# Choice of experts: two operands of the choosing arithmetic move from SBUF to PSUM

## The chip, the cores and the metric

The kernel runs on one core of a Trainium2 chip. The metric is the device time of one execution in microseconds (us). Before the change three timed runs gave 3245.78, 3250.35 and 3260.03 us, so the median is 3250.35 us. The profiled execution, from which every duration in this document comes unless another is named, took 3240.46 us; its span, from the first instruction to the last, is 3238.8 us.

Five engines work side by side, each on its own queue in program order, and meet at semaphores: PE (TensorE, matrix products), DVE (VectorE), ACT (ScalarE), POOL (GpSimd) and SP, which only issues transfers. PEld is the weight load of PE. SBUF is the working memory, PSUM the small memory into which PE writes.

## The reference

One decoder layer runs for 256 prompt tokens and 64 sample tokens: a mixer, attention over memory, and a feed-forward layer called PEER, which is where the change lies. The part of the reference that matters:

```python
q = (xt @ wq).reshape(T, PEER_HEADS, 2, PEER_HALF)          # 8 heads, 2 halves
s = jnp.einsum('thid,hikd->thik', q, sub_keys)              # 128 scores for each half
s1, i1 = lax.top_k(s[:, :, 0], K)                           # K = 16
s2, i2 = lax.top_k(s[:, :, 1], K)
comb = (s1[..., :, None] + s2[..., None, :]).reshape(T, PEER_HEADS, K * K)
cid = (i1[..., :, None] * PEER_NKEYS + i2[..., None, :]).reshape(T, PEER_HEADS, K * K)
sf, pos = lax.top_k(comb, K)
eid = jnp.take_along_axis(cid, pos, axis=-1)                # 16 of 16384 experts per head
g = jax.nn.softmax(sf, axis=-1)
act = gelu(einsum('td,tkd->tk', x, u[eid]))                 # rows of peer_u
out = einsum('tk,tkd->td', g * act, v[eid])                 # rows of peer_v
```

## The kernel before, in words

For the prompt tokens the kernel does not gather experts. It multiplies the 256 tokens with all 16384 rows of `peer_u` (the u stage, 128 row blocks of 128 experts, four units of four matrix tiles each), takes the gelu, multiplies with a gate that is zero for experts not chosen, and multiplies with all rows of `peer_v` (the v stage). For the 64 sample tokens it gathers the chosen rows and works on DVE.

**A unit of the u stage** passes four engines. DVE transposes a piece of a row block (L1837, into a tile `tt`, five of which exist), ACT rounds it to the high part `H` (L1846), POOL subtracts to get the low part `L` (L1849; a few of them are done by DVE, L1852), and PE does twelve matrix products (L1865 to L1867). Seven `H` and seven `L` tiles exist, so PE can be some units behind.

**The choice of experts** is a side task, `choose`, that runs in the first half of the u stage, between units. A stream object calls it a little at a time: after each unit it advances each side generator by its rate (0.254 steps per unit for this one), so the order of the instructions on PE, DVE, ACT and POOL is fixed when the program is written down, from counts and from a table of assumed costs (`run("dve", 2.6)` and the like), not from measured times. Only SP's order is left to a scheduler. `choose` treats three blocks of 128 rows in turn, the sample tokens (block 2) and then the two halves of the prompt (0 and 1). For each block:

- L1636 copies the key indices into PSUM as floats. L1640 and L1641 form the sums of first and second maxima, `comb`, 136 per head (the pairs that can be among the sixteen best).
- L1541 to L1549 pick the best sixteen of each head.
- L1656 to L1666 turn a position into the index of the first and of the second maximum (`pf`).
- L1668 compares each of the 128 indices of a token (8 heads of 16) with sixteen whole numbers, which gives the one-hot `oh` of 2048 elements per partition. L1672 multiplies by the key indices, L1676 sums. This happens twice per block (i = 0 and 1), six times in all.
- L1682 to L1687 form the softmax weights.

Once block 2 is done, the sample gathers start: POOL issues an indirect transfer (L1722) for each of 64 slots, and DVE takes the dot products (L1729). Once block 1 is done, the gates of the prompt begin (L1750, L1771).

`PP["n128"]`, `PP["row"]` and `PP["IF"]` are three parts of one bank of PSUM, `n128p` in the profile: the numbers 0, -1, ..., -127 in each partition, a scratch row of 128 elements, and the key indices of a block. `t8` gives one of three large tiles in SBUF, shared by `comb`, `oh` and the gathered rows `gu`. The tile `i16` (`i` in the profile) holds 0 to 15 in SBUF; the maxima `M` lie in `SS`, also in SBUF.

## Time and profile before

| | |
|---|---|
| timed runs | 3245.78, 3250.35, 3260.03 us |
| profiled execution / its span | 3240.46 / 3238.8 us |
| PE busy in the span | 3153.9 us (97%) |
| DVE, ACT, POOL busy | 2351.8, 1631.6, 1350.3 us |
| u stage (first load of a row block to last L1837) | about 1680 to 2505 us |
| `choose` (first L1640 to last L1687) | 1744.5 to 2050.5 us |

A row of the timeline gives start, duration, engine, line, operation, `out<-in`, shapes and the count of merged instructions; in brackets the idle time before it and what ended it. A row of waits gives the engine and line that waited, what it waited for, the sum in us, how often, and the longest. A row of windows gives the stretch, its length, the busy time (and instructions) of PE, PEld, DVE, ACT and POOL, the granted PE clock, the busy share of the DMA engines and GB/s. A row of a line's instructions gives min/median/max of the duration in ns.

### The profile page before, as it was taken

How to read it: one execution, taken by the hardware profiler on the slowest of the kernel's cores; microseconds unless marked ns; L12 is line 12 of the kernel's file. 1: busy time of each engine (PE TensorE's matmuls, PEld its weight loads, DVE VectorE, ACT ScalarE, POOL GpSimd, SP SyncE). 2: the span in 40 equal slices, each digit the busy share in tenths (PEclk: the TensorE clock that was granted, in tenths of full speed). 3: DMA queues.
4: the chain of work that ended last, by engine and by line, in shares of the span. 5: the costliest groups of instructions: out<-in, count | busy, mean ns of one | idle time of the engine just before them, and what ended most of it. 6: DMA issues, size and time to landing. Idle time of an engine off the chain costs nothing.

```text
span 3238.8 us, 57523 instructions
## 1 busy us (share of the span) xinstructions
PE 3153.9 (97%) x20589; PEld 2939.9 (91%) x20589; DVE 2351.8 (73%) x4548; ACT 1631.6 (50%) x3219; POOL 1350.3 (42%) x1439
## 2 busy tenths in 40 slices
PE   8999999999999999889999999999999999999997
PEld 6789999999999998869999999999999888888886
DVE  5556766666575557786687899987885788888885
ACT  5545543333454445555435444666665555555554
POOL 0011211111100001330138988988888555556653
PEclk9999999999999999999999999999999999999998
DMA  7668899888999998775786688878998999999995
GB/s 255 204 202 296 282 309 298 293 298 292 317 320 312 309 298 190 222 215 195 189 217 219 234 289 298 306 285 295 327 326 292 311 336 347 329 354 325 341 311 191
DMA packets 475371, 909.29 MB, mean 281 GB/s; under 512 B 40607, under 2 KB 286535, under 8 KB 449572
## 3 DMA queue, kind: packets, MB, share of 16 engines
q1 hardware_dynamic: 352972, 562.95, 52.5%
q0 software_dynamic: 54528, 208.44, 19.0%
q10 hardware_dynamic: 67584, 134.23, 12.2%
q8 instruction: 161, 2.64, 0.3%
q14 instruction: 126, 1.03, 0.1%
HBM read 849.41 MB, written 190.05 MB: 321 GB/s over the span
## 4 chain that ended last, share of the span: by engine, by line
PE 42%; POOL 2%; issue 2%; DVE 2%; DMA 1%; ACT 1%; SPq 0%; DVEq 0%; POOLq 0%; ACTq 0%
PE acc L2021 7%; PE acc L2022 7%; PE acc L2020 7%; PE pu L1867 6%; PE pu L1866 6%; PE pu L1865 6%; POOL L L1849 2%; PE pgate L1771 2%; DVE tt L1837 0%; PE pg L369 0%; PE pg L371 0%; PE pg L370 0%; DVE gu L1729 0%; DMA gain<-in_norm_final_dram 0%; DMA at<-act_d 0%
## 5 line engine op out<-in xcount | busy, mean ns | idle before, releaser
L251 DVE TENSOR_TENSOR L<-W,H 128x512 fp32r<-128x512 f32 x1320 | 914.1, 718 | 362.5 <-ACT H L250 346.2
L250 ACT ACTIVATE H<-W 128x512 fp32r<-128x512 f32 x1320 | 798.5, 625 | 683.9 <-PE pg L370 231.3
L1849 POOL TENSOR_TENSOR L<-tt,H 128x512 fp32r<-128x512 f32 x509 | 652.7, 1311 | 82.3 <-ACT H L1846 73.6
L1867 PE MATMUL pu<-XP,L 128*128 128x256 f32 x2048 | 582.7, 285 | 12.3 <-POOL L L1849 12.2
L369 PE MATMUL pg<-AH,H 128*128 128x320 f32 (+1 forms) x1872 | 587.9, 314 | 0.0
L1865 PE MATMUL pu<-XP,H 128*128 128x256 f32 x2048 | 585.7, 286 | 1.2 <-ACT H L1846 1.2
L1866 PE MATMUL pu<-XP,H 128*128 128x256 f32 x2048 | 579.9, 283 | 0.0
L371 PE MATMUL pg<-AH,L 128*128 128x320 f32 (+1 forms) x1872 | 579.1, 309 | 0.0
L370 PE MATMUL pg<-AL,H 128*128 128x320 f32 (+1 forms) x1872 | 578.9, 309 | 0.0
L1837 DVE STREAM_TRANSPOSE tt<-W 128x512 f32<-128x512 f32 x512 | 337.6, 690 | 115.9 <-POOL L L1849 108.4
L1867 PEld LDWEIGHTS pu<-XP,L 128*128 128x128 f32 x2048 | 392.7, 192 | 16.1 <-POOL L L1849 15.8
L2020 PE MATMUL acc<-H,wt 128*128 128x512 f32 x1024 | 398.5, 389 | 2.5 <-ACT H L250 2.5
L2021 PE MATMUL acc<-L,wt 128*128 128x512 f32 x1024 | 398.6, 389 | 0.3 <-DVE L L251 0.2
L2022 PE MATMUL acc<-H,wt 128*128 128x512 f32 x1024 | 398.4, 389 | 0.0
L1865 PEld LDWEIGHTS pu<-XP,H 128*128 128x128 f32 x2048 | 393.5, 192 | 1.6 <-ACT H L1846 1.4
L1866 PEld LDWEIGHTS pu<-XP,H 128*128 128x128 f32 x2048 | 393.2, 192 | 0.0
L1846 ACT ACTIVATE H<-tt 128x512 fp32r<-128x512 f32 x512 | 306.9, 625 | 154.9 <-DVE tt L1837 127.8
L369 PEld LDWEIGHTS pg<-AH,H 128*128 128x128 f32 (+1 forms) x1872 | 350.9, 187 | 4.5 <-issue 2.4
L370 PEld LDWEIGHTS pg<-AL,H 128*128 128x128 f32 (+1 forms) x1872 | 351.0, 188 | 2.3
L371 PEld LDWEIGHTS pg<-AH,L 128*128 128x128 f32 (+1 forms) x1872 | 350.7, 187 | 0.6
L1969 POOL TENSOR_TENSOR at<-at,G 128x108 f32<-128x108 f32 x192 | 166.6, 881 | 264.1 <-DMA at<-act_d 226.1
L2020 PEld LDWEIGHTS acc<-H,wt 128*128 128x128 f32 x1024 | 192.3, 188 | 42.7 <-ACT H L250 2.9
(489 smaller groups left out, 5334.7 us busy)
## 6 DMA issues: line engine op xcount, KB each, us to landing
u_d<-in_peer_u_dram ACTq DMA_DIRECT2D x128, 1024.0 KB
W<-u_d SPq DMA_DIRECT2D x128, 1024.0 KB
W<-in_peer_v_dram SPq DMA_DIRECT2D x256, 512.0 KB
W<-in_w_in_dram SPq DMA_DIRECT2D x176, 512.0 KB
W<-in_w_out_dram SPq DMA_DIRECT2D x64, 512.0 KB
W<-in_w_mem_k_dram SPq DMA_DIRECT2D x32, 512.0 KB
W<-in_w_mem_v_dram SPq DMA_DIRECT2D x32, 512.0 KB
W<-in_w_mem_q_dram SPq DMA_DIRECT2D x32, 512.0 KB
```

The costliest lines, as they stand in the source:

```text
L250: S.activation(h, src, AF.Copy)
L251: V.tensor_tensor(l, src, h.bitcast(F32), ALU.subtract)
L369: PE.matmul(out, hv[:, j, c0:c1], ah[:, k, 0:n], start=st, stop=False)
L370: PE.matmul(out, hv[:, j, c0:c1], al[:, k, 0:n], start=False, stop=False)
L371: PE.matmul(out, lv[:, j, c0:c1], ah[:, k, 0:n], start=False, stop=sp)
L1849: G.tensor_tensor(l, src, h.bitcast(F32), ALU.subtract)
L1865: PE.matmul(pu[:, 0:TP], hv[:, j], PP["xp"][:, 0, k], start=k == 0, stop=False)
L1866: PE.matmul(pu[:, 0:TP], hv[:, j], PP["xp"][:, 1, k], start=False, stop=False)
L1867: PE.matmul(pu[:, 0:TP], lv[:, j], PP["xp"][:, 0, k], start=False, stop=k == KC - 1)
L2020: PE.matmul(out, th, h, start=i == 0, stop=False)
L2021: PE.matmul(out, th, l, start=False, stop=False)
L2022: PE.matmul(out, tl, h, start=False, stop=i == P - 1)
```

## The change

The tile `i16` and the instruction that fills it are gone. L1668 compares with a slice of `n128` in PSUM instead; since that holds negative numbers, `pf` is formed with its sign turned (and, for i = 0, shifted by one, which the slice's start makes up for). For the sums, the sixteen second maxima of each head are first copied into the scratch row in PSUM, a new instruction per block, and L1640 and L1641 read them there. The assumed costs of the table stay as they were.

```diff
-    i16 = cst.tile([P, 16], F32, name="i16")
-    G.iota(i16, pattern=[[1, 16]], base=0, channel_multiplier=0, allow_small_or_imprecise_dtypes=True)
@@
             comb = t8("comb")[:, 0:8 * 136].rearrange("p (h n) -> p h n", h=8)
-            V.tensor_tensor(comb[:, :, 0:16], mv[:, :, 0, 0:1].broadcast_to([P, 8, 16]), mv[:, :, 1], ALU.add)
+            second = PP["row"].rearrange("p (h k) -> p h k", k=16)
+            V.tensor_copy(second, mv[:, :, 1])
+            V.tensor_tensor(comb[:, :, 0:16], mv[:, :, 0, 0:1].broadcast_to([P, 8, 16]), second, ALU.add)
             V.tensor_tensor(comb[:, :, 16:].rearrange("p h (a b) -> p h a b", b=8),
                             mv[:, :, 0, 1:].unsqueeze(3).broadcast_to([P, 8, 15, 8]),
-                            mv[:, :, 1, 0:8].unsqueeze(2).broadcast_to([P, 8, 15, 8]), ALU.add)
+                            second[:, :, 0:8].unsqueeze(2).broadcast_to([P, 8, 15, 8]), ALU.add)
@@
                 if i == 0:
                     V.tensor_copy(row, row.bitcast(U32))
-                    V.tensor_scalar(pfv, row, 1.0, -1.0, op0=ALU.max, op1=ALU.add)
+                    V.tensor_scalar(pfv, row, 1.0, -1.0, op0=ALU.max, op1=ALU.mult)
                 else:
-                    V.tensor_scalar(pfv, row, 1.0, -8.0, op0=ALU.is_gt, op1=ALU.mult)
+                    V.tensor_scalar(pfv, row, 1.0, 8.0, op0=ALU.is_gt, op1=ALU.mult)
                     V.tensor_tensor(row, row, pfv, ALU.mult)
-                    V.tensor_tensor(pfv, row, po, ALU.add)
+                    V.tensor_tensor(pfv, row, po, ALU.subtract)
                 oh = t8("oh").rearrange("p (h a b) -> p h a b", h=8, a=16)
                 V.tensor_tensor(oh, pf.unsqueeze(3).broadcast_to([P, 8, 16, 16]),
-                                i16.unsqueeze(1).unsqueeze(1).broadcast_to([P, 8, 16, 16]), ALU.is_equal)
+                                PP["n128"][:, 1 - i:17 - i].unsqueeze(1).unsqueeze(1).broadcast_to([P, 8, 16, 16]), ALU.is_equal)
```

The order of instructions on PE and ACT is the same as before. On DVE, at the place where block 1 forms its sums, the rows before the change are these (`SS` holds the maxima, `gu` a gathered row, `DOT` its dot product):

```order
L1837 STREAM_TRANSPOSE tt<-W 128x512 x4
L1852 TENSOR_TENSOR L<-tt,H 128x512
L1636 CAST n128p<-SS 128x256
L1640 TENSOR_TENSOR comb<-SS 128x8x16
L1641 TENSOR_TENSOR comb<-SS 128x8x120
L1837 STREAM_TRANSPOSE tt<-W 128x512 x2
```

With the change the same place reads as follows; lines have moved, since two were taken out near the top and two put in here (what was L1636 is L1634).

```order
L1837 STREAM_TRANSPOSE tt<-W 128x512 x4
L1852 TENSOR_TENSOR L<-tt,H 128x512
L1634 CAST n128p<-SS 128x256
L1639 COPY n128p<-SS 128x128
L1640 TENSOR_TENSOR comb<-SS,n128p 128x8x16
L1641 TENSOR_TENSOR comb<-SS,n128p 128x8x120
L1837 STREAM_TRANSPOSE tt<-W 128x512 x2
```

One copy has come in, and both sums now have one source in PSUM. Blocks 2 and 0 show the same. On SP the order has moved at one place of the u stage, where the stores of the gelu's results (`act_d`) and the loads of row blocks (`W`) alternate. Before:

```order
L1873 DMA act_d<-at 128x256
L1819 DMA W<-u_d_97 128x2048
L1873 DMA act_d<-at 128x256 x2
L1819 DMA W<-u_d_97 128x2048
L1873 DMA act_d<-at 128x256
```

With the change (the numbers in the names of tensors are two lower throughout):

```order
L1873 DMA act_d<-at 128x256 x2
L1819 DMA W<-u_d_95 128x2048
L1873 DMA act_d<-at 128x256
L1819 DMA W<-u_d_95 128x2048
L1873 DMA act_d<-at 128x256
```

The two stores that follow each other do so one row block earlier, so one load has been put behind one store.

## The prediction

> **What bounds the kernel now.** I read the page's busy times first, then the busy times in stretches of the u stage, then PE's waits, and then the timelines of DVE, POOL and PE around each wait. The columns of a stretch are its length, the busy time of PE, PEld, DVE, ACT and POOL, the granted clock, DMA share and GB/s.
>
> ```profile
> PE 3153.9 (97%) x20589; PEld 2939.9 (91%) x20589; DVE 2351.8 (73%) x4548; ACT 1631.6 (50%) x3219; POOL 1350.3 (42%) x1439
> ...
> 1800.00:1850.00 50.00, 50.00 (x419) 50.00 (x418) 42.48 (x79) 25.35 (x48) 46.29 (x36) 1.00 0.67 226
> 1900.00:1950.00 50.00, 45.08 (x364) 43.83 (x364) 47.98 (x89) 25.32 (x47) 47.35 (x38) 1.00 0.85 296
> 1950.00:2000.00 50.00, 47.39 (x388) 46.57 (x387) 48.22 (x146) 20.77 (x39) 44.38 (x37) 1.00 0.85 314
> 2000.00:2050.00 50.00, 44.46 (x349) 43.10 (x348) 48.15 (x74) 20.03 (x37) 43.23 (x35) 0.97 0.75 268
> ...
> 2100.00:2200.00 100.00, 100.00 (x846) 100.00 (x845) 81.37 (x158) 63.87 (x157) 85.51 (x70) 1.00 0.79 286
> ...
> PE pu L1867 <- POOL L L1849: 12.2, 14, 2.4
> PE pu L1865 <- ACT H L1846: 1.2, 1, 1.2
> ...
> PE acc L2020 <- ACT H L250: 2.5, 1, 2.5
> ```
>
> PE is the bound over the whole, but not from 1900 to 2057 us. There DVE is busy for 144.4 of 150 us (47.98 + 48.22 + 48.15) while PE loses time. The first two rows of waits are all of PE's waits between 1740 and 2060 us: 12.2 + 1.2 = 13.4 us in 15 waits. The last is the one wait of size after 2060 us, at the change to the v stage; so what PE gains here is kept to the end. Of the three blocks that are chosen, only the last two fall into this stretch; under block 2, from 1744 to 1836 us, PE never waits (all 15 waits end after 1900 us, and the stretch from 1800 to 1850 us has PE busy throughout), so nothing saved there counts.
>
> **What DVE is late with.** In pairs: an instruction that the change touches, POOL's run of subtractions at that moment (merged, with its count), and PE's wait a little later.
>
> ```profile
> 1889.52 6.24 DVE L1668 TENSOR_TENSOR oh<-pf,i 128x2048 f32<-128x2048 f32 x1
> 1889.83 3.77 POOL L1849 TENSOR_TENSOR L<-tt,H 128x512 fp32r<-128x512 f32 x3
> 1902.58 0.39 PE L1867 MATMUL pu<-XP,L 128*128 128x256 f32 x1 [2.36 <-POOL L L1849]
> ...
> 1949.21 4.43 DVE L1640 TENSOR_TENSOR comb<-SS 128x128 f32<-128x128 f32 x1
> 1948.47 5.02 POOL L1849 TENSOR_TENSOR L<-tt,H 128x512 fp32r<-128x512 f32 x4
> 1960.92 0.39 PE L1867 MATMUL pu<-XP,L 128*128 128x256 f32 x1 [1.73 <-POOL L L1849]
> ...
> 2003.41 7.95 DVE L1668 TENSOR_TENSOR oh<-pf,i 128x2048 f32<-128x2048 f32 x1
> 2002.92 6.29 POOL L1849 TENSOR_TENSOR L<-tt,H 128x512 fp32r<-128x512 f32 x5
> 2012.72 1.27 POOL L1849 TENSOR_TENSOR L<-tt,H 128x512 fp32r<-128x512 f32 x1 [3.52 <-ACT H L1846]
> 2012.70 0.38 PE L1865 MATMUL pu<-XP,H 128*128 128x256 f32 x1 [1.20 <-ACT H L1846]
> 2014.05 0.49 PE L1867 MATMUL pu<-XP,L 128*128 128x256 f32 x1 [0.85 <-POOL L L1849]
> 2017.58 0.38 PE L1867 MATMUL pu<-XP,L 128*128 128x256 f32 x1 [0.69 <-POOL L L1849]
> ```
>
> These are not long computations, they are waits inside the instruction. POOL's run ends at 1889.83 + 3.77 = 1893.60, and L1668 ends 2.16 us later; POOL's run ends at 2002.92 + 6.29 = 2009.21, and L1668 ends 2.15 us later; the sum L1640 ends 0.15 us after POOL's run. So a DVE instruction with both sources in SBUF stood until POOL had nothing ready, and then ran. While it stands, no `tt` is made, ACT and then POOL run dry (the 3.52 us), and PE waits. The Trainium skill, "SBUF — State Buffer", section "Who interferes with whom", says that a DVE instruction with two SBUF inputs contends with a GpSimd instruction that reads SBUF, and that the one which is first holds the shared pair for that instruction; the trace agrees on who meets whom, but DVE stood through up to five POOL instructions, not one.
>
> It also goes the other way. When DVE gets in, POOL stands:
>
> ```profile
> 1913.65 2.85 DVE L1668 TENSOR_TENSOR oh<-pf,i 128x2048 f32<-128x2048 f32 x1
> 1911.80 8.33 POOL L1849 TENSOR_TENSOR L<-tt,H 128x512 fp32r<-128x512 f32 x5 [0.56 <-ACT H L1846]
> 1917.68 0.39 PE L1867 MATMUL pu<-XP,L 128*128 128x256 f32 x1 [1.39 <-POOL L L1849]
> ...
> 2028.65 2.79 DVE L1668 TENSOR_TENSOR oh<-pf,i 128x2048 f32<-128x2048 f32 x1
> 2026.74 7.08 POOL L1849 TENSOR_TENSOR L<-tt,H 128x512 fp32r<-128x512 f32 x4 [0.50 <-ACT H L1846]
> 2032.62 0.39 PE L1867 MATMUL pu<-XP,L 128*128 128x256 f32 x1 [1.40 <-POOL L L1849]
> 2037.05 0.38 PE L1867 MATMUL pu<-XP,L 128*128 128x256 f32 x1 [1.29 <-POOL L L1849]
> ...
> 2010.00:2015.00 5.00, 2.95 (x20) 2.55 (x19) 5.00 (x12) 1.26 (x2) 1.27 (x1) 0.92 0.29 70
> 2015.00:2020.00 5.00, 4.31 (x29) 4.01 (x29) 5.00 (x6) 2.37 (x5) 4.71 (x5) 0.74 0.93 320
> ```
>
> Five subtractions took 8.33 us and four took 7.08, against 6.29 for five above: about 2 us each were lost to DVE. The last two rows show a further cost: after the longest stall the granted clock fell to 0.92 and 0.74, which is 5 × 0.08 + 5 × 0.26 = 1.7 us of PE.
>
> **The change part by part.** First the prices (a line's row gives min/median/max in ns; the group rows from 1889 to 2057 us end in the mean of one in ns).
>
> ```profile
> L1672 DVE TENSOR_TENSOR oh<-oh,n128p x6: 2241/2244/2249, 1801.8 to 2036.2; 128x2048 f32<-128x2048 f32 x6
> L1665 DVE TENSOR_TENSOR n128p<-n128p,pf 128x128 f32<-128x128 f32 x3 | 0.9, 299 | 0.1
> 1948.89 0.42 DVE L1636 CAST n128p<-SS 128x256 f32<-128x256 uint32 x1
> 1953.57 1.15 DVE L1641 TENSOR_TENSOR comb<-SS 128x960 f32<-128x960 f32 x1
> L1849 POOL TENSOR_TENSOR L<-tt,H 128x512 fp32r<-128x512 f32 x100 | 130.6, 1336 | 12.9 <-ACT H L1846 12.5
> L1722 POOL DMA_INDIRECT gu<-in_peer_u_dram,EID x18 | 17.3, 959 | 8.5 <-DVE DOT L1729 5.0 <-PE pu L1867 1.8 <-issue 1.3
> L1682 DVE TENSOR_TENSOR GA<-SF 128x128 f32<-128x128 f32 x2 | 1.1, 551 | 0.0
> L1687 DVE TENSOR_TENSOR GA<-GA,gs 128x128 f32<-128x128 f32 x2 | 0.9, 446 | 0.1
> L1852 DVE TENSOR_TENSOR L<-tt,H 128x512 fp32r<-128x512 f32 x2 | 1.3, 670 | 0.3 <-ACT H L1846 0.3
> 1843.67 5.18 SPq L1873 DMA_DIRECT2D act_d<-at  x2
> ```
>
> *The one-hot, L1668.* Its new form has one source in SBUF and one in PSUM, as L1672 has, with the same 2048 elements. L1672 took 2.24 to 2.25 us in all six cases, POOL busy or not. Four instances lie where PE waits: 6.24 + 2.85 + 7.95 + 2.79 = 19.83 us becomes 4 × 2.25 = 9.0, so 10.8 us less on DVE.
>
> *The first sums, L1640.* 128 elements with a source in PSUM cost 0.30 us by L1665. Of the three instances one counts, the one at 1949 us: 4.43 becomes 0.30, 4.1 us less.
>
> *The copy* is new. Half of L1636's size from SBUF to PSUM: at least 0.15, at most 0.42 us; 0.30 by L1665, which is nearest in size. It does not stand behind POOL: L1636 itself ran in 0.42 us at 1948.89, inside the very run of POOL that held L1640 for 4 us. The Trainium skill, same page and section, speaks against this part: a copy can enter a mode that takes the shared pair. With that the copy at 1949 would stand as L1640 did and the 4.1 us would be lost again; the section refers to conditions, and L1636's row is against it.
>
> *The second sums, L1641*, keep 1.15 us (they ran right behind L1640). Behind a freed L1640 they could have met POOL themselves, but their second source is now in PSUM too.
>
> *Sign changes* swap one arithmetic operation for another in the same instructions: nothing. *The iota* leaves POOL's queue before the first matrix product, 1.8 ms ahead of the stretch in question; I take nothing for it. *SP's order*: the pair of stores moves to where a load now goes first; in the trace of before the second store of the pair was held about 5 us (the SP row), so a load could come up to 5 us later, yet three row blocks fit in the buffers and a block feeds PE for four units. I take nothing; were it not hidden, a few us once.
>
> DVE's sum from 1889 to 2057 us: 10.8 + 4.1 − 0.3 = 14.6 us less, so 144.4 of 150 us becomes about 130. That is enough to remove DVE as the bound, but DVE's own sum is not PE's gain; that is capped by what PE lost.
>
> *PE's gain.* I count the waits that follow directly on one of these meetings: 2.36 + 1.73 + 1.20 + 0.85 + 0.69 + 1.39 + 1.40 + 1.29 = 10.9 us. The other seven of the 15, each under 0.5 us, make 2.5 us; I leave them, since POOL has little room: 100 × 1.27 us (a subtraction undisturbed) + 17.3 for gathers are 144 us, against 168 − 13.4 − 1.7 = 153 us that PE needs for the same stretch, 6% of room less the gaps around the gathers. The clock dip goes with the stall at 2003 us: 1.7. Together **12.6 us**. Bounds: all waits, the dip, and the restart of the PE pipe after each of 15 stalls (0.1 us, 0.39 against 0.28 for a product) give 13.4 + 1.7 + 1.5 = 16.6 us; if only the three long standings go, 6.8 + 1.7 = 8.5 us.
>
> The sum against its own time is 3240.46 − 12.6 = 3227.9 us. The median of the runs shown lies 9.9 us above the profiled execution; since I cannot say what makes that up, I carry it along: 3250.35 − 12.6, about **3238 us**.
>
> **The rivals.**
>
> *More goes than I count.* With no stall, PE's reserve of finished tiles never empties and the small waits go too; unprofiled runs, which spread by 14 us, may also stand longer than the profiled one. Gain 16.6 us or more: 3234 us and below.
>
> *The remaining meetings take over, in part.* L1682, L1687 and L1852, six instances in the stretch, keep both sources in SBUF. They took 0.55, 0.45 and 0.67 us, so in this trace none stood long; but where they fall against POOL's runs shifts. One long standing costs PE what the one at 2003 us did, 1.20 + 0.85 + 0.69 + 1.7 = 4.4 us. With one or two of them the gain is 4 to 8 us: 3242 to 3246 us.
>
> *Slower.* The same mechanism at its full price: all six stand through a whole run, 6 × 4.4 = 26.4 us, against 15.1 us taken away: 11 us slower, 3262 us. It turns from gain to loss at the fourth standing (17.6 us). For it speaks only that POOL's runs get longer when nothing of DVE interrupts them; against it, six of six passed.
>
> *It does not do what it says.* If the long L1668 waited for something other than POOL (a buffer of the shared tiles), the operand's place is of no account, and the time stays 3250 us. The two ends of L1668 that follow the ends of POOL's runs by 2.16 and 2.15 us are against it.
>
> **How the numbers follow.** Forecast 0.55, its own range 8.5 to 16.6 us of gain, 3234 to 3242 us; more goes 0.17; taken over in part 0.17; no effect 0.08; slower 0.03. The range reaches down to the whole 16.6 us from the profiled execution's time, 3224 us, and up to no effect, 3252 us. A measurement of this kernel tells about 0.5% from no change, that is 16.3 us, so even a right forecast is within it: faster by over 0.5% needs the first rival, or a good part of the spread of the medians (0.12 from it, 0.15 from the forecast), 0.27; slower by over 0.5% needs the last two with a bad spread, 0.03; the rest, 0.70, is no change that can be told.
>
> **What would show it.** L1668 (its new form) at 2.2 to 2.3 us six times; L1640 at 0.3; the copy at 0.3 or below, also inside a run of POOL; POOL's five subtractions at 6.3 us, not 8.3, around L1668; DVE at 85 to 90% from 1900 to 2050 us; PE's waits on L1849 and L1846 down from 13.4 to about 2.5 us; clock 1.00 throughout the stretch. I am wrong if L1668 still varies, if L1682 or L1852 shows 4 us or more, if POOL's gathers or a load become what PE waits for, or if the waits go and the end does not move with them.

## The result and the profile after

With the change the kernel took 3220.82 us (median of six runs, 3218.64 to 3225.40) where the kernel before took 3248.23 us (six runs beside them). The ratio is 0.9918, 95% interval 0.9906 to 0.9930: 27.4 us less. That is outside the predicted range and on the side of the first rival, "more goes than I count". Repeated on two other occasions, the same comparison gave 0.9932 (0.9906 to 0.9958) and 0.9927 (0.9906 to 0.9947), by the medians 19.0 and 22.3 us.

The profiled execution after took 3218.82 us, its span is 3217.0 us. Lines have moved: L1846, L1849, L1865, L1867 and L1668 to L1687 keep their numbers, lines ahead of `choose` are two lower. First the engines, the product that opens each group of three in the u stage (its last two numbers with a point are the first and the last start), PE's waits from 1740 to 2060 us, and the stretches in which DVE was full before:

```profile
PE 3147.9 (98%) x20589; PEld 2939.2 (91%) x20589; DVE 2339.4 (73%) x4551; ACT 1633.9 (51%) x3219; POOL 1333.5 (41%) x1438
...
L1865 PE MATMUL pu<-XP,H x2048: 274/283/386, 1694.8 to 2499.2; 128*128 128x256 f32 x187
...
PE pu L1867 <- POOL L L1849: 3.5, 5, 1.8
...
1900.00:1950.00 50.00, 49.38 (x408) 48.77 (x407) 47.91 (x109) 25.83 (x49) 46.27 (x39) 1.00 0.90 316
1950.00:2000.00 50.00, 50.00 (x417) 49.94 (x416) 47.96 (x136) 22.62 (x44) 47.91 (x40) 1.00 0.90 326
2000.00:2050.00 50.00, 46.95 (x382) 45.91 (x381) 48.47 (x91) 26.78 (x52) 45.12 (x38) 1.00 0.80 302
```

The same product in the profile before:

```profile
L1865 PE MATMUL pu<-XP,H x2048: 274/283/420, 1700.1 to 2518.2; 128*128 128x256 f32 x187
```

The u stage, measured between these two starts, takes 2499.2 - 1694.8 = 804.4 us, where it took 818.1 us: 13.7 us less. It also begins 5.3 us earlier, which nothing in the prediction accounts for. What lies behind it (3217.0 - 2499.2 = 717.8 us against 3238.8 - 2518.2 = 720.6 us) is 2.8 us shorter. PE's waits fell from 13.4 to 3.5 us and the granted clock is 1.00 throughout. But DVE is as busy as before, 144.3 of 150 us against 144.4.

The touched instructions after:

```profile
L1639 DVE COPY n128p<-SS x3: 295/295/295, 1739.4 to 1938.9; 128x128 f32<-128x128 f32 x3
L1640 DVE TENSOR_TENSOR comb<-SS,n128p x3: 286/286/286, 1739.7 to 1939.3; 128x128 f32<-128x128 f32 x3
L1668 DVE TENSOR_TENSOR oh<-pf,n128p x6: 2286/2287/2289, 1790.6 to 2009.0; 128x2048 f32<-128x2048 f32 x6
L1682 DVE TENSOR_TENSOR GA<-SF x3: 548/733/3083, 1824.1 to 2027.6; 128x128 f32<-128x128 f32 x3
```

All prices of the prediction came out: the one-hot 2.29 us six times, the first sums and the copy 0.29 and 0.30 us. New is the last row: L1682, which still has both sources in SBUF, once took 3.08 us. Such a wait inside a DVE instruction, behind POOL, is called a standing below. The timelines of DVE and POOL at three places show why some stand and others do not:

```profile
1938.06 6.32 POOL L1849 TENSOR_TENSOR L<-tt,H 128x512 fp32r<-128x512 f32 x5
1938.95 0.29 DVE L1639 COPY n128p<-SS 128x128 f32<-128x128 f32 x1
1939.28 0.29 DVE L1640 TENSOR_TENSOR comb<-SS,n128p 128x128 f32<-128x128 f32 x1
...
2006.29 6.32 POOL L1849 TENSOR_TENSOR L<-tt,H 128x512 fp32r<-128x512 f32 x5
2008.96 2.29 DVE L1668 TENSOR_TENSOR oh<-pf,n128p 128x2048 f32<-128x2048 f32 x1
2014.56 0.96 POOL L1722 DMA_INDIRECT gu<-in_peer_u_dram,EID  x1 [1.95 <-DVE DOT L1729]
...
2024.23 6.29 POOL L1849 TENSOR_TENSOR L<-tt,H 128x512 fp32r<-128x512 f32 x5
2027.60 3.08 DVE L1682 TENSOR_TENSOR GA<-SF 128x128 f32<-128x128 f32 x1
```

The copy, the first sums and the one-hot all ran inside a run of five subtractions without standing, and the run took 6.3 us, not 8.3. L1682 ended at 2030.68, 0.16 us after the run that it met (2024.23 + 6.29 = 2030.52). The largest wait that PE has left (1.8 us, between 2015 and 2020 us) comes from another place: POOL stood 1.95 us at a gather, whose buffer a dot product of DVE had not yet freed.

### The profile page after: what moved, and what is told of

It is laid out like the page before. It is cut to its first block, busy times and chain, and to the rows that moved or that the text cites. A ratio compares the mean times of both kernels' runs of the same rounds, so it can differ in the third digit from the quotient of the medians.

```text
span 3217.0 us, 57525 instructions
## 1 busy us (share of the span) xinstructions
PE 3147.9 (98%) x20589; PEld 2939.2 (91%) x20589; DVE 2339.4 (73%) x4551; ACT 1633.9 (51%) x3219; POOL 1333.5 (41%) x1438
## 4 chain that ended last, share of the span: by engine, by line
PE 44%; DVE 2%; POOL 1%; issue 1%; DMA 1%; ACT 1%; SPq 0%; DVEq 0%; POOLq 0%; ACTq 0%
PE acc L2021 7%; PE acc L2022 7%; PE acc L2020 7%; PE pu L1867 7%; PE pu L1865 7%; PE pu L1866 7%; PE pgate L1771 2%; POOL L L1849 1%; DVE tt L1837 0%; PE pg L367 0%; PE pg L369 0%; PE pg L368 0%; DVE gu L1729 0%; DMA at<-act_d 0%; ACT junk L2054 0%
## 5 line engine op out<-in xcount | busy, mean ns | idle before, releaser
L1849 POOL TENSOR_TENSOR L<-tt,H 128x512 fp32r<-128x512 f32 x509 | 645.9, 1299 | 75.9 <-ACT H L1846 67.1
L1865 PE MATMUL pu<-XP,H 128*128 128x256 f32 x2048 | 585.6, 286 | 0.0
L1867 PE MATMUL pu<-XP,L 128*128 128x256 f32 x2048 | 580.6, 283 | 3.7 <-POOL L L1849 3.5
L2020 PE MATMUL acc<-H,wt 128*128 128x512 f32 x1024 | 398.4, 389 | 0.0
L1867 PEld LDWEIGHTS pu<-XP,L 128*128 128x128 f32 x2048 | 392.7, 192 | 5.4 <-POOL L L1849 5.3
L1865 PEld LDWEIGHTS pu<-XP,H 128*128 128x128 f32 x2048 | 393.1, 192 | 0.2 <-ACT xs L1503 0.2
L1846 ACT ACTIVATE H<-tt 128x512 fp32r<-128x512 f32 x512 | 306.8, 625 | 135.3 <-DVE tt L1837 101.5
L1969 POOL TENSOR_TENSOR at<-at,G 128x108 f32<-128x108 f32 x192 | 151.9, 805 | 259.5 <-DMA at<-act_d 195.1
L2021 PEld LDWEIGHTS acc<-L,wt 128*128 128x128 f32 x1024 | 192.2, 188 | 41.0 <-DVE L L249 1.2
```

Of the source, the lines that this page charges most:

```text
L1849: G.tensor_tensor(l, src, h.bitcast(F32), ALU.subtract)
L1865: PE.matmul(pu[:, 0:TP], hv[:, j], PP["xp"][:, 0, k], start=k == 0, stop=False)
L1867: PE.matmul(pu[:, 0:TP], lv[:, j], PP["xp"][:, 0, k], start=False, stop=k == KC - 1)
L2020: PE.matmul(out, th, h, start=i == 0, stop=False)
L2021: PE.matmul(out, th, l, start=False, stop=False)
```

## The experiments

Fifteen runs. Each ratio is to the kernel before on the same occasion, with its 95% interval. "u stage" is the time between the first and the last start of the product above.

### Which part of the change carries the gain

Four kernels, run together, took the change apart. The first is the change with the sums undone:

```diff
-            second = PP["row"].rearrange("p (h k) -> p h k", k=16)
-            V.tensor_copy(second, mv[:, :, 1])
-            V.tensor_tensor(comb[:, :, 0:16], mv[:, :, 0, 0:1].broadcast_to([P, 8, 16]), second, ALU.add)
+            V.tensor_tensor(comb[:, :, 0:16], mv[:, :, 0, 0:1].broadcast_to([P, 8, 16]), mv[:, :, 1], ALU.add)
...
-                            second[:, :, 0:8].unsqueeze(2).broadcast_to([P, 8, 15, 8]), ALU.add)
+                            mv[:, :, 1, 0:8].unsqueeze(2).broadcast_to([P, 8, 15, 8]), ALU.add)
```

> The whole change took 27.4 us off the median. This is the change with the sums undone: the one-hot reads the whole numbers from PSUM, the sums read both sources from SBUF again, the copy is gone, and SP's order is that of before. Theory 1 (what counts are the standings of DVE behind POOL's subtractions): the six L1668 take 2.29 us each, an L1640 may stand again (4.4 us at block 1 in the trace of before, which cost PE 1.7 us), so most of the gain stays, 15 to 25 us. Theory 2 (the time went with the tile and its iota, in the part of the program before the u stage, which was 5.3 us shorter in the profile after): the first product of the u stage starts at about 1695 us as after, not 1700. Theory 3 (the sums carry the gain, since the block's first instruction sets how the rest falls against POOL): under 10 us.

Measured: 3232.22 us, ratio 0.9952 (0.9936 to 0.9968). The u stage took 808.6 us, 9.5 less than before. The six comparisons took 2.29 us each, and the first sums of block 1 stood 4.45 us again. The sign that theory 2 named tells nothing: the first product of the u stage came at 1699.2 us here, without the tile, and at 1698.5 us in the third kernel below, also without it.

The second is the opposite, the kernel before with the copy and the sums in PSUM:

```diff
+            second = PP["row"].rearrange("p (h k) -> p h k", k=16)
+            V.tensor_copy(second, mv[:, :, 1])
-            V.tensor_tensor(comb[:, :, 0:16], mv[:, :, 0, 0:1].broadcast_to([P, 8, 16]), mv[:, :, 1], ALU.add)
+            V.tensor_tensor(comb[:, :, 0:16], mv[:, :, 0, 0:1].broadcast_to([P, 8, 16]), second, ALU.add)
...
-                            mv[:, :, 1, 0:8].unsqueeze(2).broadcast_to([P, 8, 15, 8]), ALU.add)
+                            second[:, :, 0:8].unsqueeze(2).broadcast_to([P, 8, 15, 8]), ALU.add)
```

> The kernel before with the copy and the sums' second source in PSUM; tile, iota and one-hot as before. Theory 1: L1640 at 0.29 us three times, while the L1668 still stand now and then (2.3 to 8 us); gain 2 to 8 us. Theory 2: first product of the u stage at about 1700 us as before. Theory 3: 15 us or more.

Measured: 3243.77 us, ratio 0.9980 (0.9965 to 0.9995), u stage 814.0 us, 4.1 less than before. The u stage of the two halves adds up: 9.5 + 4.1 = 13.6 us against 13.7 for the whole change. Theory 3 falls. The first product of the u stage came at 1706.1 us, 6 us later than expected.

The third differs from the change in the place of one operand only:

```diff
-                                PP["n128"][:, 1 - i:17 - i].unsqueeze(1).unsqueeze(1).broadcast_to([P, 8, 16, 16]), ALU.is_equal)
+                                n128[:, 1 - i:17 - i].unsqueeze(1).unsqueeze(1).broadcast_to([P, 8, 16, 16]), ALU.is_equal)
```

> The change in everything (tile and iota gone, sums, sign changes), but the one-hot takes its numbers from the copy of n128 that lies in SBUF: it differs from the change in the place of that one operand alone. Theory 1: L1668 varies again from 2.3 to 8 us, time near that of the sums alone, 20 to 25 us above the change. Theory 2: the beginning stays short, first product of the u stage at about 1695 us, and about 5 us of the gain stays beside that of the sums. That the place of the operand is of no account: the time of the change, L1668 at 2.29 us.

Measured: 3239.31 us, ratio 0.9970 (0.9957 to 0.9984), u stage 815.0 us. Its one-hot:

```profile
L1668 DVE TENSOR_TENSOR oh<-pf,n x6: 2796/2960/7940, 1794.3 to 2022.8; 128x2048 f32<-128x2048 f32 x6
```

With the operand in SBUF the one-hot stands again, up to 7.94 us, and the u stage is 10.6 us longer than with the change. The whole was 18.5 us above the change's first median, less than the 20 to 25 that theory 1 expected. This settles that it is the place of the operand, not the sign changes or the order on the queues (which is that of the change here), that counts.

The fourth puts the removed tile back, unused:

```diff
+    i16 = cst.tile([P, 16], F32, name="i16")
+    G.iota(i16, pattern=[[1, 16]], base=0, channel_multiplier=0, allow_small_or_imprecise_dtypes=True)
     n128 = cst.tile([P, P], F32, name="n128")
```

> The change, with the tile of sixteen numbers and the iota that fills it put back, unused: everything behind it lies 64 bytes higher in each partition of SBUF, and POOL has one instruction more at the start. Theory 1, with the 5.3 us at the beginning as chance: the time of the change within 3 us. Theory 2 (the beginning): 5 us above the change, first product of the u stage at about 1700 us instead of 1695.

Measured: 3229.22 us, ratio 0.9939 (0.9921 to 0.9956), u stage 803.1 us. The u stage keeps its gain, but the time is above the change's (by the ratios of its three comparisons, 0.0007 to 0.0021, that is 2 to 7 us), and the first product of the u stage comes at 1702.9 us. With this the beginning became a question of its own, taken up below.

### The two kernels again, and block 2

The change unaltered, for its size and for a second trace:

> The change itself, unaltered, on another occasion and beside the others. Its first six runs gave 3220.8 us, 27.4 us below before; but the u stage, from its first product to the last, is only 13.7 us shorter in the profile after (804.4 against 818.1 us), and the change with the unused tile put back gained 18.5 us by its median with a u stage of 803.0 us. Theory 1 (only the u stage is changed; what comes before and behind it varies from execution to execution by some 10 us each, and the first six runs had luck): gain of 14 to 18 us, 3230 to 3234 us where before is at 3248. Theory 2 (the tile and its iota cost something of their own): again 25 us or more, and the first product of the u stage at 1695 us again, not 1698 to 1706.

Measured: 3225.67 us beside 3244.64, ratio 0.9932 (0.9906 to 0.9958). The u stage took 804.3 us again and began at 1695.7 us. The gain of 19.0 us lies between the two theories, above the 14 to 18 of the first and below the 25 of the second.

The kernel before, unaltered:

> The kernel before, unaltered, for a second trace of it. Its first profiled execution (3240.5 us) lies 7 us below the median of its 28 runs. Theory 1 (the standings repeat from run to run, the rest of the program varies): L1668 of block 1 at 7.9 us and L1640 of block 1 at 4.4 us again, u stage 818 us within 1 us, and the difference of the whole before or behind the u stage, most of it in the granted clock. Rival (the standings vary, and the first profile showed few of them): other lengths of L1668 and L1640, and a u stage that is longer by what the whole is longer.

Measured: 3244.23 us, ratio to itself 0.9988 (0.9967 to 1.0008), u stage 818.2 us. The rows of its one-hot and its first sums:

```profile
L1668 DVE TENSOR_TENSOR oh<-pf,i x6: 2814/2953/7942, 1794.3 to 2027.2; 128x2048 f32<-128x2048 f32 x6
L1640 DVE TENSOR_TENSOR comb<-SS x3: 425/848/4460, 1742.9 to 1947.7; 128x128 f32<-128x128 f32 x3
```

The longest standing is 7.94 us in this trace and was 7.95 in the first, the first sums 4.46 and 4.43. The meetings of these two lines are not a matter of chance: the order of the instructions is written down, and the long ones repeat in every trace of a kernel that has them. The rival, that other executions stand longer, found nothing to rest on in this second trace; executions that were not profiled cannot be seen.

The change for block 2 alone:

```diff
-            second = PP["row"].rearrange("p (h k) -> p h k", k=16)
-            V.tensor_copy(second, mv[:, :, 1])
+            second = PP["row"].rearrange("p (h k) -> p h k", k=16) if tb == 2 else mv[:, :, 1]
+            if tb == 2: V.tensor_copy(second, mv[:, :, 1])
...
-                                PP["n128"][:, 1 - i:17 - i].unsqueeze(1).unsqueeze(1).broadcast_to([P, 8, 16, 16]), ALU.is_equal)
+                                (PP["n128"] if tb == 2 else n128)[:, 1 - i:17 - i].unsqueeze(1).unsqueeze(1).broadcast_to([P, 8, 16, 16]), ALU.is_equal)
```

> The change for block 2 (the sample rows) alone: blocks 0 and 1 read both operands of the one-hot and of the sums from SBUF, without the copy. The prediction said that nothing saved under block 2 counts, since PE never waits there. If so the u stage takes 818 us as before, within 1.5 us, with L1668 of blocks 0 and 1 between 2.8 and 8 us. If block 2 matters (DVE that gets ahead under it has a reserve for the next blocks), the u stage is some us shorter.

Measured: 3243.60 us, ratio 0.9993 (0.9972 to 1.0013), u stage 818.2 us: nothing saved under block 2 counts, as predicted.

### One step on

The change, and the two instructions of the softmax weights with one source in PSUM:

```diff
-            V.tensor_tensor(GA, SF, SF[:, :, 0:1].broadcast_to([P, 8, 16]), ALU.subtract)
+            top, gs = PP["row"][:, 0:8], PP["row"][:, 8:16]
+            V.tensor_copy(top, SF[:, :, 0])
+            V.tensor_tensor(GA, SF, top.unsqueeze(2).broadcast_to([P, 8, 16]), ALU.subtract)
             S.activation(GA, GA, AF.Exp)
-            gs = small([P, 8], "gs")
```

> The change and one step on: the two remaining instructions of the softmax weights with both sources in SBUF (L1682, the subtraction of the largest, and L1687, the product with the reciprocal) get one source in PSUM; the largest of each head is first copied there, one more instruction per block, and the sums gs are formed there. In the profile after L1682 stood 2.5 us once (3.08 us at 2027.6), and PE still waited 3.5 us in the u stage, 1.8 in one piece. Theory 1: L1682 and L1687 at 0.3 us each time, u stage 802 to 804 us, so 0 to 2.5 us below the change, which the medians may not tell. Rival (the standing is only passed to the next instruction with two SBUF sources, L1852 or the dot products): u stage as with the change, and a standing elsewhere.

Measured: 3222.52 us, ratio 0.9926 (0.9897 to 0.9956), beside the change's 0.9932; the u stage took 802.8 us, the shortest of all. Its three instructions and all of PE's waits from 1740 to 2060 us:

```profile
L1683 DVE COPY n128p<-SF x3: 145/145/149, 1825.0 to 2028.4; 128x8 f32<-128x8 f32 x3
L1684 DVE TENSOR_TENSOR GA<-SF,n128p x3: 288/289/289, 1825.2 to 2028.6; 128x128 f32<-128x128 f32 x3
L1688 DVE TENSOR_TENSOR GA<-GA,n128p x3: 286/286/289, 1830.3 to 2031.1; 128x128 f32<-128x128 f32 x3
...
PE pu L1868 <- POOL L L1850: 2.5, 4, 1.7
```

The standing of L1682 is gone and no other took its place. In time it cannot be told from the change. PE has only 2.5 us of waits left in this stretch, so little more is to be had here.

### Standing, or DVE's time as such?

The prediction held that DVE would no longer be the bound. The busy share said otherwise. Two kernels make each comparison twice, once with the first of the two in SBUF, once with both in PSUM:

```diff
+                V.tensor_tensor(oh, pf.unsqueeze(3).broadcast_to([P, 8, 16, 16]),
+                                n128[:, 1 - i:17 - i].unsqueeze(1).unsqueeze(1).broadcast_to([P, 8, 16, 16]), ALU.is_equal)
                 V.tensor_tensor(oh, pf.unsqueeze(3).broadcast_to([P, 8, 16, 16]),
                                 PP["n128"][:, 1 - i:17 - i].unsqueeze(1).unsqueeze(1).broadcast_to([P, 8, 16, 16]), ALU.is_equal)
```

> The change, with each one-hot comparison made twice: first with the numbers in SBUF, then, over it, with those in PSUM as in the change. Six instructions more on DVE, each a meeting with POOL. Theory 1 (standing behind POOL costs, DVE's own work does not as long as it is some 2 us apiece): these six stand as those of before, 2.8 to 8 us, and the u stage goes back to 818 us or above, since 9.2 us of PSUM comparisons in the stretch come on top: 818 to 826 us. Rival (DVE is full anyway, 144.3 of 150 us from 1900 to 2050 us after the change, so any work more costs PE its length): like the control with the numbers in PSUM, plus only the excess of the standing.

The control has `PP["n128"]` in place of `n128` in the added lines.

> The control: the change, with each one-hot comparison made twice, both times with the numbers in PSUM. Six instructions more on DVE of 2.29 us each, four of them in the stretch from 1875 to 2035 us, 9.2 us there, and no meeting. Theory 1: DVE has a reserve of finished tiles, PE loses little, u stage 804 to 807 us. Rival (DVE is full in the stretch, so its work counts one for one): u stage 811 to 814 us.

Measured with the added comparison in SBUF: 3245.30 us, ratio 0.9995 (0.9979 to 1.0011), u stage 823.3 us. With both in PSUM: 3231.64 us, ratio 0.9956 (0.9926 to 0.9985), u stage 813.3 us. The control's product and PE's waits:

```profile
L1867 PE MATMUL pu<-XP,H x2048: 274/283/416, 1693.7 to 2507.1; 128*128 128x256 f32 x187
...
PE pu L1869 <- POOL L L1851: 6.9, 4, 3.8
PE pu L1867 <- ACT H L1848: 1.4, 2, 0.7
```

Four comparisons of 2.29 us, 9.2 us of plain DVE work without any standing, made the u stage 8.9 to 9.9 us longer than the change's 804.4 to 803.4 in its three traces. Theory 1's reserve does not exist; the rival is right, DVE is full there. And these standings cost what they add to DVE's time, no more: the four added in SBUF took 6.29 + 2.86 + 7.95 + 2.80 = 19.9 us on DVE and cost 18.9 to 19.9.

All 17 traces, with those of the kernels that are told of further below, fall on one line. For each, the DVE time from block 0's first comparison on (comparisons, first sums and copy of block 1, and the subtractions, products and copies of the softmax weights of blocks 0 and 1), and the u stage:

| kernel | DVE time of these, us | u stage, us | difference |
|---|---|---|---|
| each comparison twice, SBUF first | 31.6 | 823.3 | 791.7 |
| before with the tile twice as wide | 28.7 | 819.1 | 790.4 |
| before, two traces, and with the tile behind `W` | 26.3, 26.3, 26.4 | 818.1, 818.2, 818.1 | 791.8, 791.9, 791.7 |
| change in block 2 alone | 26.3 | 818.2 | 791.9 |
| change, one-hot from SBUF | 24.8 | 815.0 | 790.2 |
| sums alone | 22.5 | 814.0 | 791.5 |
| each comparison twice, PSUM | 20.9 | 813.3 | 792.4 |
| one-hot alone | 18.0 | 808.6 | 790.6 |
| change, three traces | 14.1, 14.1, 11.7 | 804.4, 804.3, 803.4 | 790.3, 790.2, 791.7 |
| change with the tile kept, two traces, and with its room alone | 11.8, 11.7, 11.7 | 803.1, 803.4, 803.3 | 791.3, 791.7, 791.6 |
| change and weights | 11.2 | 802.8 | 791.6 |

Over 20 us of DVE time the difference stays between 790.2 and 792.4 us: a microsecond of DVE in this stretch is about a microsecond of the end, whether DVE computes or stands. Kernels with SP's order of before and with that of the change lie on the same line, so that SP's order was rightly put at nothing, to within the 2 us that the line leaves. There is one exception to the rule of one for one. Traces of one kernel differ by whether L1682 of block 1 stands: in two of the three traces of the change it took 3.08 and 3.10 us, in the third 0.54. There the u stage was only 0.9 to 1.0 us shorter. The five traces in which it stands (the two of the change, the one-hot alone, the one-hot from SBUF, the tile twice as wide) are the five with a difference of 790.2 to 790.6 us; all others have 791.3 or more. This last standing of 2.5 us, at the end of the stretch, costs about 1 us.

### The beginning: the tile's place

So far the traces part into two groups in the stage that projects the memory (up to 208 us): one with the tile in place, one without. Its three products per tile of weights (L320 to L322, two lines lower without the tile) stream 512 columns of `H` or `L` each. Between 80 and 200 us the first of the three, L320, has these busy times and counts before (columns: stretch, its length, PE's busy time and count, PEld's, clock, DMA share, GB/s):

```profile
80.00:200.00 120.00, 64.30 (x161) 30.06 (x160) 1.00 0.62 197
```

And after:

```profile
80.00:200.00 120.00, 65.03 (x163) 30.43 (x163) 1.00 0.61 191
```

PE is busy throughout in both, and yet 120 us hold 160 or 161 of these products with the tile and 163 without. From the start of one product to the start of the next, called the pace here, it is 232 ns and 229 ns (medians over the three lines). Two kernels ask whether it is the tile's room or its iota. The change with an unused tile of the same size, and no iota:

```diff
+    pad = cst.tile([P, 16], F32, name="pad")
     n128 = cst.tile([P, P], F32, name="n128")
```

> The traces so far part into two groups in the stage that projects the memory, 80 to 200 us: with the tile of sixteen numbers in place one product follows the other after 232 ns (median, lines L320 to L322, four traces), without it after 229 ns (six traces), and the stage ends 2.8 us later with it. This kernel is the change with an unused tile of 64 bytes per partition where the tile was, and no iota. Theory A (what counts is where the tiles behind it lie in SBUF, 64 bytes past a multiple of 128 or at one): 232 ns, last product of the stage at 206.5 to 208.2 us, as before. Theory B (the iota on POOL counts): 229 ns, 203.8 to 205.1 us, as with the change. The u stage takes 803 to 804.5 us either way.

Measured: 3232.68 us, ratio 0.9953 (0.9930 to 0.9977), u stage 803.3 us. The pace is 232 ns and the stage's last product comes at 207.9 us. Its row:

```profile
80.00:200.00 120.00, 64.19 (x160) 30.06 (x160) 1.00 0.61 191
```

So it is the room, not the iota. The kernel before with a tile twice as wide:

```diff
-    i16 = cst.tile([P, 16], F32, name="i16")
+    i16 = cst.tile([P, 32], F32, name="i16")[:, 0:16]
```

> The kernel before, with its tile of sixteen numbers made 128 bytes wide per partition (of which 64 are used), the iota kept: everything behind it lies at multiples of 128 bytes again, as in the change, but 128 bytes higher. Theory A (place against multiples of 128): 229 ns from product to product, the memory stage ends at 203.8 to 205.1 us. Theory B (iota, or that there is a tile at all): 232 ns and 206.5 us or more. The u stage takes 818 us either way, with L1668 of block 1 at 7.9 us and L1640 of block 1 at 4.4 us, since one-hot and sums are those of before.

Measured: 3246.66 us, ratio 1.0001 (0.9986 to 1.0016), u stage 819.1 us, with the standings of before (7.95 and 4.45 us). The pace is 233 ns, and the row counts 160 again; the last product comes at 206.2 us. Theory A falls in its form: a shift by 128 bytes is as bad as one by 64, so multiples of 128 are not what counts. Of theory B the iota had just fallen with the run before; that any tile there is enough fits both runs. What stays is that the arrangement without the tile is the better one. Whether a larger multiple counts was not tried.

The last question was whose place it is:

```diff
-    i16 = cst.tile([P, 16], F32, name="i16")
-    G.iota(i16, pattern=[[1, 16]], base=0, channel_multiplier=0, allow_small_or_imprecise_dtypes=True)
...
     wroom = cst.tile([P, 1024 * WB], F32, name="W")
+    i16 = cst.tile([P, 16], F32, name="i16")
+    G.iota(i16, pattern=[[1, 16]], base=0, channel_multiplier=0, allow_small_or_imprecise_dtypes=True)
```

> The kernel before, with the tile of sixteen numbers and its iota taken after the weights' buffer W instead of ahead of it: W lies where the change has it, while the tiles H and L, which PE reads, and all behind them lie 64 bytes higher, as before. Theory A1 (the place of W, which transfers write and ACT and DVE read, sets the pace of the memory stage): 229 ns from product to product and an end at 203.8 to 205.4 us. Theory A2 (the place of H and L, which PE reads): 232 ns and 206.5 to 208.2 us. The u stage takes 818 us, with the standings of before.

Measured: 3243.44 us, ratio 0.9996 (0.9980 to 1.0013), u stage 818.1 us. Its row:

```profile
80.00:200.00 120.00, 64.30 (x161) 30.06 (x160) 1.00 0.57 188
```

The pace is 232 ns with `W` where the change has it, so it is the place of `H` and `L`, or of a tile behind them, that sets it. The end of the stage, 205.7 us, lies between the two expectations and tells nothing.

The place of `H` and `L` alone is not enough. The v stage streams 512 columns of the same `H` and `L` tiles, and there the pace is 227 ns in all 17 traces, with the tile or without. The first of its three products (L2020), before and then after, between 2600 and 3000 us:

```profile
2600.00:3000.00 400.00, 228.84 (x589) 110.42 (x589) 1.00 0.95 338
...
2600.00:3000.00 400.00, 228.87 (x589) 110.36 (x588) 1.00 0.96 341
```

What differs in the memory stage is open. Its weights `MH` and `ML`, which PE loads, also lie behind the tile; no run moves them by themselves.

Its price in time, on one chip, the change with the tile and the change itself:

> The change with the unused tile and its iota, a second time, beside the change itself. If the tile's place is the rest of the gain: 4 to 6 us above the change, as the first products of the u stage suggest (1701 to 1703 us with the tile, 1694 to 1699 without it). If the rest is chance: within 2 us of the change.

> The change itself, a third time. From the parts shown so far: 14 us of the u stage and 3 to 6 us of the tile's place, so 17 to 20 us below before (it was 27.4 and 19.0 us by the medians of the first two). If there is a cost of before that no trace has shown yet (executions in which the standings are longer): 22 us or more again.

Measured with the tile: 3226.78 us (3221.95 to 3232.13), ratio 0.9945 (0.9923 to 0.9966). Without: 3220.74 us (3218.62 to 3224.41), ratio 0.9927 (0.9906 to 0.9947). The u stage took 803.4 us in both. The medians differ by 6.0 us, the ratios by 0.0018, 5.8 us. The change itself lies 22.3 us below before. That is above the 17 to 20 us expected and at the mark set for a cost of before that no trace has shown; the interval of the ratio, 17 to 30 us, decides for neither. Of the 6 us the memory stage accounts for about half: its last product comes at 206.1 and 203.3 us here. Over all traces it comes at 203.3 to 205.6 us with `H` and `L` in the place of the change (nine traces), at 205.7 to 208.7 otherwise (eight), 2.6 us apart on average. At the first product of the u stage the same two groups are 4.1 us apart (1695.7 and 1699.8 us on average). Where the rest arises was not found.

The other comparisons bear the 6 us out. Take the gain of each run's median over before on its occasion, and subtract the gain of its u stage over 818.1 us. What is left is 1.1 to 13.7 us, 6.5 on average, in the nine comparisons with `H` and `L` in the place of the change, and -2.8 to 3.5 us, 0.1 on average, in the six others. The spread within each group shows that the 6 us are no sharp figure. The three lowest of the nine, 1.1 (the change in block 2 alone), 4.5 and 5.3 us, are kernels in which comparisons of blocks 0 and 1 still stand, so a further cost of the standings of a few us, outside the u stage, is not excluded.

## Why the prediction was wrong

*What bounds the kernel.* Right that the stretch from 1900 to 2057 us decides the u stage, that block 2 does not count (u stage 818.2 us with the change there alone), and that PE's gain is kept: behind the u stage, before and after take 717.8 to 725.4 us in five traces, without order.

*The mechanism.* Right for the standings. One operand's place makes the one-hot stand up to 7.94 us or never. The Trainium skill, "SBUF — State Buffer", section "Who interferes with whom", states that the engine which is first keeps the pair for the whole instruction; the traces go beyond that, as the prediction had noted: they show a standing of the same 7.94 to 7.95 us, through five subtractions and not one, in all eight traces of kernels that compare in SBUF.

*The prices.* L1668 at 2.29 us (2.25 predicted), L1640 at 0.29, the copy at 0.30, inside a run of POOL. The objection drawn from the same section of the Trainium skill, that a copy may take the pair, did not come to pass: it took 295 ns in all three cases, also 0.9 us into a run of 6.32 us.

*PE's gain, first failed step.* "DVE's own sum is not PE's gain; that is capped by what PE lost." The sum on DVE was 14.6 us, and the u stage became 13.7 us shorter in the first trace of the change, 14.7 us in the third, in which L1682 does not stand, against the 12.6 predicted. The size was within the bounds that were given, but the reasoning failed: "DVE at 85 to 90%" was expected, and DVE stayed at 96%. The doubled comparisons show it directly, since 9.2 us of plain DVE work lengthened the u stage by 8.9 to 9.9 us. What was overlooked stands in the group of DVE's transposes, one per unit (count, then busy time and mean). Before, from 1889 to 2057 us (168 us):

```profile
L1837 DVE STREAM_TRANSPOSE tt<-W 128x512 f32<-128x512 f32 x102 | 64.8, 679 | 1.9 <-POOL L L1849 1.8
```

After, from 1874 to 2037 us (163 us):

```profile
L1837 DVE STREAM_TRANSPOSE tt<-W 128x512 f32<-128x512 f32 x108 | 68.8, 682 | 2.1 <-POOL L L1849 2.0
```

The time freed was filled with the next units at once: 108 tiles in 163 us instead of 102 in 168. These two stretches do not hold the same side work; counted from the first comparison of block 0 to the last L1687 of block 1, it is 96 tiles in both, in 161.4 us before, 148.3 us in the first trace of the change and 147.1 in the third. DVE, which sets the pace here, stays full when it gets faster; what changes is how much it gets done. Of the seven small waits (2.5 us) that the prediction left standing for want of room on POOL, some went too: PE's 3.5 us that remain are five waits, four small ones of 1.7 us in all and one of 1.8 us that goes back to the gather. That a gather becomes what PE waits for was one of the prediction's signs of being wrong, and this much of it showed. Two of the small ones, 1.2 us, follow the standing of L1682 and are missing in the third trace.

*The edits costed at nothing, second failed step, and the larger miss.* The prediction took nothing for the iota, since it "leaves POOL's queue before the first matrix product". That looked at the instruction that goes, and not at the 64 bytes of its tile. They move `H`, `L` and all that lies behind them, and PE's products in the memory stage went from 232 to 229 ns apart; in all, the tile's place costs about 6 us by the direct comparison, of which the traces place 2.6 in the memory stage. Why the place counts there stays open. With it the change is worth 14 to 15 + 6 = 20 to 21 us, against 19.0, 22.3 and 27.4 us measured. The range was drawn from the u stage alone, so its lower end, 3224 us, missed, by 3 us. That it missed is in part chance: on the second occasion the change's median, 3225.67 us, would have lain inside.

*The offset.* The 9.9 us between the profiled execution and the median were carried along. On the five occasions the kernel before had medians from 3243.0 to 3248.2 us, single runs from 3234 to 3269 us; the profiled one of 3240.5 us was one of the shorter. The u stage is the same in both its traces (818.1 and 818.2 us), so this scatter lies before and behind it. Three runs had made the median of before 3250.35 us, and the first comparison of six and six runs came out larger than both repeats; what of its 27.4 us goes beyond 20 to 21 is put down to that, which is argued, not shown.

*The rivals.* The first one had the right direction, and some of the small waits did go, as it said. But the u stage gained 13.7 to 14.7 us, less than its 16.6, and the second trace of before stood no longer than the first; what it lacked was the tile. The second one, that the remaining meetings take over, happened in two of three traces (L1682, 2.5 us longer), at about 1 us instead of 4.4. No effect fell with the kernel whose one-hot reads the same numbers from SBUF and stands, slower with the time itself.

## What to carry to other kernels

Where DVE works beside subtractions of POOL, look for DVE instructions of two SBUF sources whose duration varies from one instance to the next, and give one source a place in PSUM, if need be by a copy. In a stretch in which an engine is 96% busy, as DVE is here, count the time it spends, standing or computing, one for one, and expect its busy share to stay; a standing at the end of the stretch may cost less. When a tile is added or removed, compare the pace of the products in stages that the change does not touch: what lies behind the tile moves with it.

## What was not expected of the hardware

The place in SBUF of `H`, `L` and the tiles behind them changed the pace of the memory stage's products of 512 columns, 232 against 229 ns, with PE busy throughout in both and the granted clock at 1.00; moved by 64 or 128 bytes, they are about equally slow (232 and 233 ns). The v stage, which streams 512 columns of the same `H` and `L`, kept its 227 ns in all traces. The u stage, whose products stream 256 columns of another tile, kept its length with the tile or without (803.1 to 804.4 us). And the standings of L1668 and L1640 repeat to a few hundredths of a microsecond from trace to trace (those of L1682 do not), while single runs of the kernel before spread by 17 to 33 us on one occasion.
